# A depthwise convolution's taps on TensorE: one full product per tap, or four products of 32 channels for four taps, on shifted copies

## The chip, the core and the metric

The program runs on one core of a Trainium2 chip. The metric is the time of one execution on the device in microseconds (us), from start to end; less is better. A core has TensorE (PE in the rows; its weight loads are PEld), VectorE (DVE), ScalarE (ACT), GpSimd (POOL) and SyncE (SP), each with its own instruction stream, and DMA queues that move data between DRAM and the on-chip memories SBUF and PSUM, both of 128 partitions.

## The reference

Four layers (A, B, C, D) run one after the other on 336 tokens: 64 of a running stream and 272 of a new one. The change is in layer D, a Conformer convolution module of 2048 channels with 31 taps, and in the step that ends the program.

```python
def conformer_mixer(u, w_in, conv_w, conv_b, ln_g, ln_b, w_out, buf):
    a, b, g = jnp.split(u @ w_in, 3, axis=-1)
    v = a * jax.nn.sigmoid(b)
    ext = jnp.concatenate([buf.astype(v.dtype), v], axis=1)
    new_buf = ext[:, -(D_CONV - 1):]
    c = causal_dwconv(ext, conv_w, conv_b)      # 31 taps, each channel by itself
    c = jax.nn.silu(layernorm(c, ln_g, ln_b))
    y = (c * jax.nn.silu(g)) @ w_out
    return y, new_buf
# trunk: x = x + rmsnorm(y, norm_post)
```

## The kernel before

All activations are held with channels on partitions and tokens along the free dimension. A projection tile (`in_tile`) makes 128 output channels for all 336 tokens: 8 blocks of the contraction, three products each (high and low parts of weights and activations), 24 products of 128x128 by 336 columns. Each of these weight groups of 128x1024 is loaded by SP's queue into `wraw` (three buffers), rounded into `whi` by ScalarE, and its remainder `wlo` is taken by VectorE, or by GpSimd for the groups that the table `PRM["lo"]` names; `whi` and `wlo` have five buffers. A call of `tick` in the program prepares the weight group that lies some three tiles ahead.

Layer D has 16 channel tiles j of 128 channels. Iteration j of its loop makes tile `db` (ScalarE takes a tanh of it into `sig`) and tile `da`; VectorE multiplies them into `ext[j % 7]` (`dext` in the rows), which holds both streams with 30 earlier columns each, so that a convolution output has T = 366 columns. Then the loop puts TensorE's part of the convolution of tile j-2 (`conv_pe`), and as many gate tiles `dg` as `PRM["g"][j]` says. The 31 taps of a tile are split over three engines:

- TensorE takes the first `npe(j)` taps. For each, ScalarE writes a diagonal matrix (`diag`, identity times the tap), and TensorE multiplies it with a shifted window of `ext` into a PSUM tile `cv`. The operands are f32, and the rows show two passes (a weight load and a product record) for each such product.
- GpSimd takes the next `ngt(j)` taps: ScalarE scales a window (`gp` for the first, `gq` for the others), GpSimd adds them up in `gp` (`conv_pool`).
- VectorE takes the rest, in place on `cv` (`conv_dve`, a pair of tiles interleaved), then adds `gp`.

`finish` adds the bias (ScalarE, `call`) and squares (`sq`), and GpSimd sums both over the tiles into `s1`, `s2`, which two pairs of products with `onesE` turn into the layernorm's mean and square mean. After the 16 iterations stand the convolutions of tiles 14 and 15 and the remaining gate tiles; of these, 13 is made before the layernorm sums and 14 and 15 after them. What VectorE and ScalarE's taps advance at each place is set by the tables `PRM["pump"]`, `PRM["act"]` and `PRM["t"]`, so each engine's order is fixed in the program; engines wait for one another by semaphores.

The program ends in `outproj`, branch `last`: the sum of squares of the projected output gives `rstd` (ScalarE, a logarithm and an exponential), and VectorE and GpSimd compute `yg * rstd` and `x + yg` for 8 blocks, each of which SP then stores.

Layer A holds a place that will be needed: five products in a row of 128x32 matrices, which go to PSUM partitions r to r+32 in w columns, the last with 16 columns:

```python
for e, (r, c, w) in enumerate(((0, 32, 32), (0, 128, 32), (64, 192, 32), (0, 256, 32), (64, 320, 16))):
    self.mm(a[r:r + 32, c:c + w], k3[:, t, e], q3[:, t, e, :w])
```

Of the kernel before, what the change touches and what calls it, by code (L numbers as in the profile page):

```python
# [10 lines left out]
F32 = mybir.dt.float32  # L11
# [33 lines left out]
    "npe": [5, 5, 6, 6, 4, 4, 6, 3, 7, 5, 2, 6, 9, 4, 14, 5],  # L45
    "ngt": [3, 4, 6, 9, 6, 11, 6, 9, 7, 9, 8, 13, 8, 12, 4, 10],
    "act": [1, 16, 4, 77, 3],
    "pump": [[5, 10, 6, 3, 4], [6, 5, 6, 2, 7]],
# [158 lines left out]
def constants():  # L207
# [11 lines left out]
    for h in range(2):  # L219
# [6 lines left out]
        "k_tri": chunk_mask(),  # L226
    }


def pack(w, layers):  # L230
# [16 lines left out]
    a["dh"] = w["state_conformer_conv"][0, 0].T.reshape(16, 128, 30).transpose(1, 0, 2)  # L247
    lat = w["cache_mla_latent"][0, 0]
# [100 lines left out]
class Trunk:  # L349
# [161 lines left out]
    def outproj(self, i, layer, ready, close):  # L511
# [22 lines left out]
        with ExitStack() as st:  # L534
# [56 lines left out]
            if last:  # L591
                r = self.rstd(S["s"], D)
# [29 lines left out]
            if last:  # L622
                def scale(k, e):
                    e.tensor_tensor(yg[:, k], yg[:, k], r, op=OP.mult)
# [5 lines left out]
                for k in (6, 7):  # L630
                    scale(k, G)
                scale(0, V)
                scale(5, V)
                for k in range(5):
                    if k < 4:
                        scale(k + 1, V)
                    new_x(k, V)
                    if k in (1, 2, 3):
                        new_x((6, 7, 5)[k - 1], G)
                return  # L640
# [797 lines left out]
    def layer_d(self, i):  # L1438
        nc, tc, V, A, G = self.nc, self.tc, self.V, self.A, self.G
        T = 366  # L1440
        with ExitStack() as st:
# [15 lines left out]
            NPT = 8  # L1457
# [3 lines left out]
            NX = 7  # L1461
            npe = lambda j: PRM["npe"][j]
# [6 lines left out]
            V.tensor_scalar(dw, self.col("dcw", 0, DTAP * 16), 0.5, None, op0=OP.mult)  # L1469
            onesE = cp.tile([128, 128], F32, name="onesE")  # L1470
# [10 lines left out]
            def diags(j, n0):  # L1481
                d = wk.tile([128, NPT, 128], F32, name="diag")
                for n in range(n0, min(n0 + NPT, npe(j))):
                    A.activation(d[:, n - n0], self.ident, AF.Copy, scale=tap(n, j))  # L1484
                    yield
                cv[j, "dg", n0] = d
# [7 lines left out]
            def conv_pe(j):  # L1494
                c = cv[j] = pp["c"].tile([128, 512], F32, name="cv")
                for n0 in range(0, npe(j), NPT):
                    while (j, "dg", n0) not in cv:
                        pump_act(1)
                    d = cv.pop((j, "dg", n0))
                    for n in range(n0, min(n0 + NPT, npe(j))):  # L1500
                        self.mm(c[:, :T], d[:, n - n0], ext[j % NX][:, n:n + T], n == 0, n == npe(j) - 1)

# [199 lines left out]
```

## Time and profile before

| | |
|---|---|
| time before, median of 3 runs | 1330.7 us (1330.37 to 1334.92) |
| profiled execution, its own time | 1332.71 us |
| its span, first to last instruction | 1330.9 us |
| PE, DVE, ACT, POOL busy, share of the span | 95%, 70%, 62%, 26% |
| mean granted TensorE clock | 0.987 |

The profile is one execution; what its rows add up to is set against its span. Busy shares are means over all four layers; layer D's convolution takes only the stretch from 1016 to 1243 us, and its shares are read there.

### The profile page before, as it was taken

Reading aid. Unit: us, or ns where it says so; the run is one execution under the profiler, and the core shown is the slowest. Engines: PE = TensorE matmul, PEld = TensorE weight load, DVE = VectorE, ACT = ScalarE, POOL = GpSimd, SP = SyncE. Lnnn points to the kernel's source line nnn. Section 1 sums busy time; section 2 is a strip of 40 time slices with the busy share of each in tenths; the row PEclk is TensorE's granted clock in tenths of the full one; section 3 lists DMA queues with packets and bytes.
Section 4 is the critical chain, followed back from the end, with each engine's and each line's share of the span. In section 5 each row is a group of like instructions: output and inputs, shape, how many; then the busy total and the mean of one; then the engine's idle time right before and its main releaser. Section 6 shows DMA issues by size and latency. Waiting matters only on the chain.

```text
span 1330.9 us, 21343 instructions
## 1 busy us (share of the span) xinstructions
PE 1261.2 (95%) x8100; PEld 1194.0 (90%) x8100; DVE 932.3 (70%) x1727; ACT 818.8 (62%) x1560; POOL 339.6 (26%) x376
## 2 busy tenths in 40 slices
PE   5999999999999999899979999998999999999995
PEld 4999999999999999799979898887998899887895
DVE  5676666676658999956755555555647799989683
ACT  4677666667545877764554544454544878778653
POOL 0000000000002122100040000000012899999794
PEclk9999999999999999899999999899999999999998
DMA  5433333433441444344343222221342233322341
GB/s 202 134 113 110 124 119 106 137 123 103 135 143 64 145 142 141 112 144 143 110 155 104 88 88 90 77 96 40 120 142 81 94 112 111 111 96 80 100 147 64
DMA packets 48247, 151.29 MB, mean 114 GB/s; under 512 B 6432, under 2 KB 11888, under 8 KB 48144
## 3 DMA queue, kind: packets, MB, share of 16 engines
q1 hardware_dynamic: 44880, 142.70, 32.5%
q0 software_dynamic: 1504, 5.04, 1.2%
q10 hardware_dynamic: 1760, 2.19, 0.5%
q8 instruction: 63, 1.03, 0.3%
q14 instruction: 40, 0.33, 0.1%
HBM read 145.45 MB, written 4.46 MB: 113 GB/s over the span
## 4 chain that ended last, share of the span: by engine, by line
PE 60%; DVE 11%; ACT 9%; POOL 9%; issue 5%; DMA 2%; POOLq 0%; DVEq 0%; ACTq 0%
PE acc L389 33%; PE bacc L389 10%; POOL gp L1511 5%; PE o L389 3%; PE hacc L389 3%; DVE wlo L330 2%; POOL wlo L330 2%; PE y L389 2%; ACT whi L318 2%; PE sp L389 2%; DMA wraw<-in_wts_dram 2%; ACT Pp L1379 2%; PE ss L389 2%; PE misc L389 1%; PE x L389 1%
## 5 line engine op out<-in xcount | busy, mean ns | idle before, releaser
L389 PE MATMUL acc<-uh,whi 128*128 128x336 f32 x1208 | 391.2, 324 | 1.1 <-ACT vv L908 1.1
L389 PE MATMUL acc<-uh,wlo 128*128 128x336 f32 x1208 | 383.1, 317 | 5.1 <-POOL wlo L330 5.1
L389 PE MATMUL acc<-ul,whi 128*128 128x336 f32 x1208 | 382.1, 316 | 0.0
L318 ACT ACTIVATE whi<-wraw 128x1024 fp32r<-128x1024 f32 (+2 forms) x267 | 273.3, 1028 | 93.2 <-DMA wraw<-in_wts_dram 59.4
L330 DVE TENSOR_TENSOR wlo<-wraw,whi 128x1024 fp32r<-128x1024 f32 (+2 forms) x229 | 288.0, 1272 | 32.9 <-ACT whi L318 28.3
L389 PEld LDWEIGHTS acc<-uh,wlo 128*128 128x128 f32 x1208 | 226.7, 188 | 5.9 <-POOL wlo L330 5.9
L389 PEld LDWEIGHTS acc<-uh,whi 128*128 128x128 f32 x1208 | 227.5, 188 | 4.2 <-ACT vv L908 1.6
L389 PEld LDWEIGHTS acc<-ul,whi 128*128 128x128 f32 x1208 | 227.7, 189 | 2.0
L1519 DVE SCALAR_TENSOR_TENSOR cv<-dext,dw,cv 128x366 f32<-128x366 f32 x280 | 146.0, 595 | 0.7
L1511 POOL TENSOR_TENSOR gp<-gp,gq 128x366 f32<-128x366 f32 x109 | 115.9, 1064 | 22.9 <-ACT gq L1510 8.9
L614 POOL TENSOR_TENSOR x<-x,sroot 128x336 f32<-128x336 f32 x6 | 5.2, 893 | 448.6 <-ACT sroot L602 393.1
L330 POOL TENSOR_TENSOR wlo<-wraw,whi 128x1024 fp32r<-128x1024 f32 (+1 forms) x38 | 88.9, 2345 | 102.9 <-DVE sump L544 83.2
L389 PE MATMUL bacc<-oh,whi 128*128 128x336 f32 x288 | 92.1, 320 | 0.0
L389 PE MATMUL bacc<-oh,wlo 128*128 128x336 f32 x288 | 91.3, 317 | 0.0
L389 PE MATMUL bacc<-ol,whi 128*128 128x336 f32 x288 | 91.1, 316 | 0.0
L1510 ACT ACTIVATE gq<-dext,dw 128x366 f32<-128x366 f32 x109 | 61.6, 595 | 25.7 <-POOL gp L1511 25.4
L389 PE MATMUL acc<-oh,whi 128*128 128x336 f32 x192 | 62.2, 324 | 2.4 <-ACT dsg L1671 1.4
L389 PE MATMUL acc<-ol,whi 128*128 128x336 f32 x192 | 62.1, 323 | 2.4 <-DVE ol L1655 1.2
L389 PE MATMUL acc<-oh,wlo 128*128 128x336 f32 x192 | 61.7, 321 | 1.9 <-DVE wlo L330 1.8
L389 PE MATMUL cv<-dext,diag 128*128 128x366 f32 x182 | 59.0, 472 | 1.0 <-ACT diag L1484 0.9
L1379 ACT ACTIVATE Pp<-sp,mx 64x80 f32<-64x80 f32 (+4 forms) x80 | 30.0, 376 | 45.9 <-DVE mx L1377 26.0
L1228 POOL DMA_DIRECT2D uv<-in_wts_dram x8 | 5.7, 718 | 199.5 <-DVE sg L1132 117.8
(421 smaller groups left out, 2653.5 us busy)
## 6 DMA issues: line engine op xcount, KB each, us to landing
wraw<-in_wts_dram SPq DMA_DIRECT2D x243, 512.0 KB, 3.4
wraw<-in_wts_dram SPq DMA_DIRECT2D x16, 384.0 KB, 3.1
out_hg_dram<-sf SPq DMA_DIRECT2D x16, 128.0 KB, 2.0
wraw<-in_wts_dram SPq DMA_DIRECT2D x8, 256.0 KB, 2.7
ukt<-in_ukt_dram POOLq DMA_DIRECT2D x8, 256.0 KB, 3.0
uv<-in_wts_dram POOLq DMA_DIRECT2D x8, 256.0 KB, 4.3
x<-in_x_dram SPq DMA_DIRECT2D x8, 168.0 KB, 5.7
out_y_dram<-x SPq DMA_DIRECT2D x8, 168.0 KB, 1.9
```

Of the source, the lines that this page charges most:

```text
L318: self.nc.scalar.activation(hi[:, :n], self.raw[i][:, :n], AF.Copy)
L330: e.tensor_tensor(lo[:, :n], self.raw.pop(i)[:, :n], hi[:, :n].bitcast(F32), op=OP.subtract)
L389: self.PE.matmul(out, l, r, start=start, stop=stop)
L614: G.tensor_tensor(self.x[:, k], self.x[:, k], sq, op=OP.mult)
L1228: nc.gpsimd.dma_start(uv, src[:, :, 256 * (p % 2):256 * (p % 2) + 256])
L1379: A.activation(P[r0:r1, c:c + n], s[r0:r1, c:c + n], AF.Exp, scale=C_SCALE, bias=mx[r0:r1, j:j + 1], accum_out=sm[r0:r1, j:j + 1])
L1510: A.activation(q, e[:, n:n + T], AF.Copy, scale=tap(n, j))
L1511: G.tensor_tensor(cv[j, "p"], cv[j, "p"], q, op=OP.add)
L1519: V.scalar_tensor_tensor(c[:, :T], ext[j % NX][:, n:n + T], tap(n, j), c[:, :T], op0=OP.mult, op1=OP.add)
```

## The change

TensorE's taps are grouped by four. For tile j, `ext` is stored to DRAM (`store`, tile `dxt`) and read back by four DMAs (`shifts`, tile `dsh`): partition block n of `dsh` (32 partitions) holds, for each of the four 32-channel groups g, those 32 channels shifted by n columns. A product then takes a 128x32 matrix (`dcw`: four 32x32 diagonals one above the other, for taps 4m to 4m+3) and `dsh[:, g, 4m:4m+366]`, and writes the 32 partitions of group g. Four products, one for each g, make a step of four taps for all 128 channels. `PRM["npm"]` gives the steps of each tile: 52 in all (208 products, the 32nd tap zero). Tile 0 keeps the diagonals, with `nd` = 11 taps. `dcw` is made by VectorE in one instruction for a tile from the identity and the taps (`tap_tiles`); the taps' tile `dtw` is loaded once by GpSimd's queue and halved by VectorE.

The tables change with it: TensorE's taps go from 91 to 219 (11 + 208), GpSimd's from 125 to 93, VectorE's from 280 to 184; gate tiles after the loop move between the convolutions of tiles 13, 14 and 15. In the last step the exponential is written twice, to PSUM for VectorE and to SBUF for GpSimd, and VectorE's intermediate product stays in PSUM.

```diff
-    "npe": [5, 5, 6, 6, 4, 4, 6, 3, 7, 5, 2, 6, 9, 4, 14, 5],
-    "ngt": [3, 4, 6, 9, 6, 11, 6, 9, 7, 9, 8, 13, 8, 12, 4, 10],
+    "npm": [0, 2, 4, 3, 3, 2, 4, 3, 4, 4, 4, 4, 4, 4, 4, 3],
+    "ngt": [5, 5, 2, 6, 4, 7, 4, 3, 7, 7, 9, 7, 3, 9, 1, 14],
...
+            def store(j):
+                z = cv[j, "dr"] = dram.tile([128, 396], F32, name="dxt")
+                nc.sync.dma_start(z, ext[j % NX][:, :396])
+
+            def shifts(j):
...
+                e = cv[j, "e"] = ec.tile([128, 4, EL], F32, name="dsh")
+                for n in range(4):
+                    nc.sync.dma_start(e[32 * n:32 * n + 32], z[:, n:n + EL].rearrange("(g c) t -> c g t", c=32))
+
+            def tap_tiles(j):
+                n = 4 * PRM["npm"][j]
+                if n == 0:
+                    d = cv[j, "w"] = ep.tile([128, PRM["nd"], 128], F32, name="diag")
+                    for n in range(PRM["nd"]):
+                        A.activation(d[:, n], self.ident, AF.Copy, scale=tap(n, j))
+                    return
+                d = cv[j, "w"] = wk.tile([128, n, 32], F32, name="dcw")
+                V.tensor_tensor(d, id32.unsqueeze(1).to_broadcast([128, n, 32]),
+                                tw[:, j, :n].unsqueeze(2).to_broadcast([128, n, 32]), op=OP.mult)
...
-                    for n in range(n0, min(n0 + NPT, npe(j))):
-                        self.mm(c[:, :T], d[:, n - n0], ext[j % NX][:, n:n + T], n == 0, n == npe(j) - 1)
+                for m in range(last + 1):
+                    for g in range(4):
+                        self.mm(c[32 * g:32 * g + 32, :T], d[:, 4 * m + g], e[:, g, 4 * m:4 * m + T], m == 0, m == last)
...
+                rp = pf.tile([128, 512], F32, name="rend", bufs=1)[:, :NT]
+                A.activation(rp, l, AF.Exp, scale=-0.5)
+                A.activation(r, l, AF.Exp, scale=-0.5)
 
                 def new_x(k, e):
-                    e.tensor_tensor(self.x[:, k], self.x[:, k], yg[:, k], op=OP.add)
+                    t = yg[:, k] if e is G else pf.tile([128, 512], F32, name="yend")[:, :NT]
+                    e.tensor_tensor(t, yg[:, k], r if e is G else rp, op=OP.mult)
+                    e.tensor_tensor(self.x[:, k], self.x[:, k], t, op=OP.add)
                     nc.sync.dma_start(self.d["y"][:, k], self.x[:, k])
...
+                for k in range(8):
+                    new_x(k, G if k in (2, 5) else V)
```

On SP's queue in layer D, before, nothing but weight loads stands until the carried state `cc` is stored:

```order
L299 DMA wraw<-in_wts_dram 128x1024 x67
L299 DMA wraw<-in_wts_dram 128x768 x3
L1614 DMA out_cc_dram<-cc 128x960
L299 DMA wraw<-in_wts_dram 128x768 x13
L299 DMA wraw<-in_wts_dram 128x1024 x4
```

In the changed kernel, the same queue around the copy of tile 3 (`dext_10612`):

```order
L303 DMA wraw<-in_wts_dram 128x1024
L1496 DMA dxt<-dext_10612 128x396
L303 DMA wraw<-in_wts_dram 128x1024
L1504 DMA dsh<-dxt 32x4x378 x4
L303 DMA wraw<-in_wts_dram 128x1024 x2
```

A store and four reads of it stand between the weight loads once for each of tiles 1 to 15; the reads wait for the store to land, and the weight loads behind them wait in the queue.

On VectorE, where iteration 4 of layer D's loop writes its `ext` tile (`dext`, from `sig` and the projection's `acc`; the brackets tell whose semaphores an instruction waits for), before:

```order
L1519 SCALAR_TENSOR_TENSOR cv<-dext_10604,dw,cv 128x366 [waits DVE_49]
L1581 SCALAR_TENSOR_TENSOR dext_10608<-sig,acc 128x272 [waits PE_49,Activation_49]
L1582 SCALAR_TENSOR_TENSOR dext_10608<-sig,acc 128x64
L1519 SCALAR_TENSOR_TENSOR cv<-dext_10605,dw,cv 128x366 [waits DVE_49]
L1519 SCALAR_TENSOR_TENSOR cv<-dext_10604,dw,cv 128x366 [waits DVE_49]
```

and in the changed kernel:

```order
L1553 SCALAR_TENSOR_TENSOR cv<-dext_10609,dw,cv 128x366 [waits DVE_49]
L1619 SCALAR_TENSOR_TENSOR dext_10613<-sig,acc 128x272 [waits PE_49,Activation_49]
L1620 SCALAR_TENSOR_TENSOR dext_10613<-sig,acc 128x64
L1515 TENSOR_TENSOR dcw<-id_10627,dtw 128x384 [waits PE_49]
L1553 SCALAR_TENSOR_TENSOR cv<-dext_10610,dw,cv 128x366 [waits DVE_49]
```

Behind `ext` VectorE now has `dcw`, which takes the buffer of `dcw` of tile j-2 (two buffers) and so waits for TensorE's convolution of tile j-2; the taps and the `wlo` of later weight groups stand behind it.

On TensorE after the loop, before, the convolutions of tiles 14 and 15 stand together, and 144 projection products (six tiles) follow:

```order
L389 MATMUL acc<-uh,wlo 128x336
L389 MATMUL cv<-dext_10604,diag 128x366 x14
L389 MATMUL cv<-dext_10605,diag 128x366 x5
L389 MATMUL acc<-uh,whi 128x336
L389 MATMUL acc<-ul,whi 128x336
```

In the changed kernel (between the pieces only projection products, 48 of them, two tiles, in the first gap and 24, one tile, in the second):

```order
L393 MATMUL acc<-uh,wlo 128x336
L393 MATMUL cv<-dsh,dcw 32x366 x16
L393 MATMUL acc<-uh,whi 128x336
...
L393 MATMUL acc<-uh,wlo 128x336
L393 MATMUL cv<-dsh,dcw 32x366 x12
L393 MATMUL acc<-uh,whi 128x336
...
L393 MATMUL acc<-uh,wlo 128x336
L393 MATMUL cv<-s_10635,onesE 128x336
L393 MATMUL cv<-s_10636,onesE 128x336
```

The convolution of tile 15 now stands one tile ahead of the layernorm sums (`cv<-s,onesE`) instead of six.

## Rows read from the trace of the kernel before

**Rows 1.** Busy time by stretch (windows): stretch, its length, each engine's busy us, clock, DMA.

```profile
1016.00:1243.00 227.00, 220.77 (x1232) 196.15 (x1230) 202.57 (x360) 173.17 (x377) 196.36 (x167) 1.00 0.30 101
```

**Rows 2.** Groups of instructions, 1010 to 1240 us: busy, mean ns | idle ahead.

```profile
L1519 DVE SCALAR_TENSOR_TENSOR cv<-dext,dw,cv 128x366 f32<-128x366 f32 x280 | 146.0, 595 | 0.7
L1511 POOL TENSOR_TENSOR gp<-gp,gq 128x366 f32<-128x366 f32 x109 | 115.9, 1064 | 22.9 <-ACT gq L1510 8.9 <-issue 7.6
L389 PE MATMUL cv<-dext,diag 128*128 128x366 f32 x182 | 59.0, 472 | 1.0 <-ACT diag L1484 0.9
L330 POOL TENSOR_TENSOR wlo<-wraw,whi 128x1024 fp32r<-128x1024 f32 x21 | 51.5, 2456 | 9.4 <-ACT whi L318 9.4
L330 DVE TENSOR_TENSOR wlo<-wraw,whi 128x1024 fp32r<-128x1024 f32 x23 | 40.2, 1746 | 10.5 <-ACT whi L318 6.3 <-POOL gp L1511 4.2
```

**Rows 3.** Waits of TensorE, 1016 to 1243 us: total, times, longest.

```profile
PE acc L389 <- POOL wlo L330: 5.1, 3, 2.0
```

**Rows 4.** Timeline of TensorE, 1049 to 1056 us: start, length, what.

```profile
1050.47 3.85 PE L389 MATMUL cv<-dext,diag 128*128 128x366 f32 x12
```

**Rows 5.** Groups of TensorE by shape in layer A, 56.849 to 56.892 us.

```profile
L389 PE MATMUL y<-q,k 128*32 128x32 f32 x2 | 0.2, 218 | 0.0
```

**Rows 6.** The same view, 56.849 to 57.022 us.

```profile
L389 PE MATMUL y<-q,k 128*32 128x32 f32 x6 | 0.3, 203 | 0.0
...
L389 PE MATMUL y<-q,k 128*32 128x16 f32 x2 | 0.2, 190 | 0.0
```

**Rows 7.** Timeline of TensorE, the same place, 56.84 to 57.56 us.

```profile
56.67 0.28 PE L389 MATMUL y<-cum,kk 128*128 128x112 f32 x1
56.88 0.74 PE L389 MATMUL y<-q,k 128*32 128x32 f32 x14
```

**Rows 8.** Timelines of POOL, DVE and PE at layer D's start.

```profile
1024.13 0.47 POOL L1466 MEMSET dext<- 128x30 f32 x7
...
1023.34 1.54 DVE L1469 TENSOR_SCALAR dw<-vec 128x496 f32<-128x496 f32 x1
...
1026.35 1.23 DVE L330 TENSOR_TENSOR wlo<-wraw,whi 128x1024 fp32r<-128x1024 f32 x1 [1.33 <-ACT whi L318]
1028.11 0.44 DVE L1581 SCALAR_TENSOR_TENSOR dext<-sig,hacc 128x272 f32<-128x272 f32 x1 [0.54 <-ACT sig L1577]
...
1029.41 0.55 PE L389 MATMUL cv<-dext,diag 128*128 128x366 f32 x1 [0.47 <-ACT diag L1484]
```

**Rows 9.** DMA issues: count, KB each, median us from issue to landing.

```profile
wraw<-in_wts_dram SPq DMA_DIRECT2D x243, 512.0 KB, 3.4
...
out_hg_dram<-sf SPq DMA_DIRECT2D x16, 128.0 KB, 2.0
...
ukt<-in_ukt_dram POOLq DMA_DIRECT2D x8, 256.0 KB, 3.0
uv<-in_wts_dram POOLq DMA_DIRECT2D x8, 256.0 KB, 4.3
```

**Rows 10.** The chain that ended last, 1215 to 1243 us.

```profile
1218.56 22.25 PE acc L389 x144
1240.81 2.41 PE cv L389 x8
```

**Rows 11.** Timelines of DVE and ACT ahead of the layernorm sums.

```profile
1235.49 0.98 DVE L1525 TENSOR_TENSOR cv<-cv,gp 128x366 f32<-128x366 f32 x2
...
1238.01 0.49 ACT L1534 ACTIVATE sq<-call 128x336 f32<-128x336 f32 x1
```

**Rows 12.** Timeline of all engines at the program's end, 1315 to 1331 us.

```profile
1318.91 2.74 DVE L624 TENSOR_TENSOR yg<-yg,rstd 128x336 f32<-128x336 f32 x3 [7.21 <-ACT rstd L422]
...
1322.79 5.53 SPq L628 DMA_DIRECT2D out_y_dram<-x  x8
...
1326.17 0.92 DVE L627 TENSOR_TENSOR x<-x,yg 128x336 f32<-128x336 f32 x2
```

**Rows 13.** Instructions of tile `cv`: form of op, ns min/median/max, starts.

```profile
L1637 DVE TENSOR_TENSOR dt<-dt,cv x16: 503/504/505, 1245.0 to 1290.9; 128x336 f32<-128x336 f32 x16
```

More of the change, by code (lines that the diff above doesn't have):

```diff
@@ L226, in constants @@
         "k_tri": chunk_mask(),
+        "k_id32": np.ascontiguousarray(np.tile(np.eye(32, dtype=f), (4, 1))),
     }
@@ L591, in outproj @@
             if last:
-                r = self.rstd(S["s"], D)
+                l, r = self.nrm.tile([128, NT], F32, name="lnss", bufs=1), self.nrm.tile([128, NT], F32, name="rstd")
+                A.activation(l, S["s"], AF.Ln, scale=1.0 / D, bias=self.eps)
             else:
@@ L622, in outproj @@
             if last:
-                def scale(k, e):
-                    e.tensor_tensor(yg[:, k], yg[:, k], r, op=OP.mult)
+                pst = ExitStack()
+                pf = self.pool(pst, "end", 2, PSUM)
+                rp = pf.tile([128, 512], F32, name="rend", bufs=1)[:, :NT]
+                A.activation(rp, l, AF.Exp, scale=-0.5)
+                A.activation(r, l, AF.Exp, scale=-0.5)
                 def new_x(k, e):
-                    e.tensor_tensor(self.x[:, k], self.x[:, k], yg[:, k], op=OP.add)
+                    t = yg[:, k] if e is G else pf.tile([128, 512], F32, name="yend")[:, :NT]
+                    e.tensor_tensor(t, yg[:, k], r if e is G else rp, op=OP.mult)
+                    e.tensor_tensor(self.x[:, k], self.x[:, k], t, op=OP.add)
                     nc.sync.dma_start(self.d["y"][:, k], self.x[:, k])
[L630 to L639, printed above, removed]
+                for k in range(8):
+                    new_x(k, G if k in (2, 5) else V)
+                pst.close()
                 return
@@ L1455, in layer_d @@
             self.psum_pools = psum_pools
-            NPT = 8
             dh = ep.tile([128, 16, 30], F32, name="dh")
@@ L1469, in layer_d @@
             V.tensor_scalar(dw, self.col("dcw", 0, DTAP * 16), 0.5, None, op0=OP.mult)
+            tw = ep.tile([128, 16, 32], F32, name="dtw")
+            id32 = ep.tile([128, 32], F32, name="id32")
+            nc.gpsimd.dma_start(tw, self.d["dtap"])
+            nc.gpsimd.dma_start(id32, self.d["k_id32"])
+            V.tensor_scalar(tw, tw, 0.5, None, op0=OP.mult)
             onesE = cp.tile([128, 128], F32, name="onesE")
@@ L1495, in conv_pe @@
                 c = cv[j] = pp["c"].tile([128, 512], F32, name="cv")
[L1496 to L1500, printed above, removed]
-                        self.mm(c[:, :T], d[:, n - n0], ext[j % NX][:, n:n + T], n == 0, n == npe(j) - 1)
+                last = PRM["npm"][j] - 1
+                d = cv.pop((j, "w"))
+                if last < 0:
+                    for n in range(PRM["nd"]):
+                        self.mm(c[:, :T], d[:, n], ext[j % NX][:, n:n + T], n == 0, n == PRM["nd"] - 1)
+                    return
+                e = cv.pop((j, "e"))
+                for m in range(last + 1):
+                    for g in range(4):
+                        self.mm(c[32 * g:32 * g + 32, :T], d[:, 4 * m + g], e[:, g, 4 * m:4 * m + T], m == 0, m == last)
             def conv_pool(j, n):
@@ L1595, in layer_d @@
                     pump(P[4])
+            store(15)
             while len(bg) > 1:
                 pump(1)
+            for n in range(PRM["tg"][0]):
+                gtile(next(ng))
+                pump(PRM["t"][1])
+            shifts(15)
             conv_pe(14)
             pump(PRM["t"][0])
-            for _ in range(PRM["tg"]):
+            for n in range(PRM["tg"][1]):
                 gtile(next(ng))
```

38 lines of the change are left out of this document (23 added, 15 removed), and 18 rows, old and new, of the table PRM.

## The prediction

> **What bounds the kernel now.** The stretch of layer D's convolution is read first, in the view by windows: from 1016 to 1243 us TensorE is busy 220.8 of 227.0 us at a granted clock of 1.00, VectorE 202.6, GpSimd 196.4, ScalarE 173.2 [rows 1]. So TensorE is the limit there, and what its own work shrinks or grows by goes into the time nearly whole, as long as VectorE, close behind, keeps up. The view of waits tells what the missing 6 us are: 5.1 us in three places where a `wlo` that GpSimd makes came late [rows 3].
>
> Then the price of the taps. The 91 taps are 182 passes [rows 2]. In a run of 12 of them the group lasts 3.85 us, the last record 0.47 us, so a pass starts every (3.85 - 0.47) / 11 = 0.307 us [rows 2, 4]. 182 x 0.307 = 55.9 us of TensorE. VectorE's 280 taps take 146.0 us, 0.521 each; GpSimd's 109 additions 1.06 each [rows 2].
>
> **TensorE's taps.** 52 steps of four products, each product with 366 columns and two passes. If the four products of a step ran one after the other, a step would cost 8 x 0.307 = 2.46 us and the four taps as much as four full products; all hangs on whether products for different groups of 32 output partitions run at once. The kernel has one place that tells: layer A's five products with 128x32 matrices, three to partitions 0 to 31 and two to partitions 64 to 95. Five products with two passes are eight passes of 32 columns and two of 16, and the two of 16 belong to the last product. Two passes have started by 56.892 us, within 15 ns of the first start at 56.88 [rows 5, 7]. By 57.022 us both 16-column passes have started but only six of eight 32-column ones [rows 6]. So the last product, for partitions 64, overtook the one before it, for partitions 0: the two groups of partitions are served side by side, and each only keeps its own order. That speaks for a step in which each of four groups has just two passes, 2 x 0.307 = 0.61 us. The trace shows two groups at once, never four. The nearest rows bound the step: 0.61 us for four at once, 0.82 for three, 1.23 for two, 2.46 for one. I take 0.61, since the two seen did not slow each other.
>
> Changing the form of the products costs too. The last 128-column-matrix pass ahead of that place starts at 56.67, has 112 columns (0.094 us at the rate above), and the first small one starts at 56.88: 0.11 us lost [rows 7]. The Trainium skill, TensorEngine Tiling (Array Packing), Key Properties, speaks against the change here: switching the tiling mode drains the engine; the row agrees, with 0.11 us. 15 tiles with two switches each: 3.3 us.
>
> After: 11 full taps, 22 x 0.307 = 6.8; 52 x 0.614 = 31.9; 3.3. Together 42.0 against 55.9: **-13.9 us**. (With 0.82 a step -3.1, with 1.23 +18.2, with 2.46 +82.)
>
> **The other engines' share.** VectorE loses 96 taps, 50.0 us. It gains 15 `dcw`, of 256 to 512 columns: between half of a 1024-column `wlo` alone (0.6 us of 1.23) and the 1.54 of the 496-column scaling [rows 8], say 12 us; four more `wlo` in this stretch at 1.75 [rows 2], 7 us. About 172 us remain. But `dcw` of tile j waits for the convolution of j-2, which TensorE runs right behind tile `da`; that is some 2.7 us from the moment `ext` can be written, less the 0.65 us of writing it: 2 us in each of 13 iterations, 26 us. 198 us of some 210: it fits on average. Iteration by iteration, the worst are those with 20 taps and no gate tile, about 13 us of VectorE against 10 of TensorE; the next one gives the 3 us back, and the `wlo` that are queued behind lie some three tiles, 11 us, ahead of use. So I charge nothing, and hold this as what goes first if I am wrong. GpSimd loses 32 taps (34 us) and five `wlo` (5 x 2.46 = 12 us), ScalarE 80 diagonals and 32 scalings; the late `wlo` of GpSimd should mostly go: **-4 us** of the 5.1 (bounds 0 and -5.1).
>
> **The start of layer D.** GpSimd issues the load of `dtw` (256 KB) only behind its seven memsets, which end at 1024.6 [rows 8]; loads of that size on its queue land 3.0 to 4.3 us after issue [rows 9], at 1027.6 to 1028.9. VectorE reaches the halving of `dtw` at 1024.9 [rows 8] and waits; queued behind are a `wlo` and `ext` of tile 0. Halving (0.8 to 1.54), memset 0.2, `wlo` 1.23, `ext` 0.65: `ext` is there at 1030.4 to 1032.5 instead of 1028.7, and TensorE's first convolution, which started at 1029.41 [rows 8], starts at 1030.5 to 1032.6. **+2.2 us**.
>
> **Ahead of the layernorm.** Before, six tiles of 3.71 us (22.25 / 6) stood behind the last convolution and covered all that VectorE, ScalarE and GpSimd still had to do: the eight passes of the sums followed without a gap [rows 10]. Now only one tile does. Count from the end of tile 14's convolution: two tiles 7.4, tile 15's three steps 2.05, one tile 3.7: TensorE is free at 13.2. VectorE takes 9 of tile 14's taps meanwhile; when tile 15's convolution ends at 9.5, 9 taps (4.7) and two additions of `gp` (0.98 [rows 11]) remain: 15.2. The last square comes 2.0 us behind these additions (1236.47 to 1238.50 [rows 11]): 17.2, and GpSimd's sums about as late. The sums then end 2 to 4 us later than TensorE alone would: **+3 us** (up to 7, if VectorE gets to tile 14 late, as its queue still holds the pair 12 and 13).
>
> **The last step.** VectorE and GpSimd worked side by side on SBUF from 1318.91 to 1327.1 [rows 12]; VectorE's first three operations took 2.74 us beside GpSimd, its last two 0.92 alone. With one operand and the intermediate in PSUM, VectorE's rows hold 503 to 505 ns while GpSimd works [rows 13]: 12 x 0.52 = 6.2 us, to 1325.1. SP issues a store each 0.69 us (5.53 / 8 [rows 12]) and keeps up. **-2 us** (0 to -3).
>
> **Sum.** -13.9 - 4 + 2.2 + 3 - 2 = -14.7 us: 1332.7 becomes 1318.0 in the profiled execution, which lay 2.0 us over the median of the runs; for the median, 1330.7 - 14.7 = 1316.0.
>
> **Rivals.** *Slower: the groups don't run four at once.* With two at a time the step is 1.23 us, the sum -14.7 + 32.1, 1348 us. The mechanism would be that products start strictly in program order: the second pass of each waits for the first in the same partitions, and the next group's product stands behind it, so that one pass starts every 0.307 us beside another's end, four times 0.307 a step. It decides from 0.90 us a step on. Against it stands the overtaking in [rows 6]. The Trainium skill, TensorE: Matmul & The Clock Gate, Part 3 (Packing small matmuls), has this very rule, strict order of the products' starts and ends; the overtaking contradicts it. The Trainium skill, same page and section, gives a measured 2.38x for three column groups; by that a step is an estimated 0.77 us and the sum -6 us, about 1324; no run here shows three.
>
> *Three at a time* (a read or issue limit that only shows beyond two): 0.82 us a step, -14.7 + 10.8, 1327 us.
>
> *Weights late.* A store of 203 KB and 774 KB of reads now stand between the weight loads of 512 KB and 3.4 us each [rows 9]. SP holds the queue while the store lands (2.0 us for 128 KB [rows 9]) and issues five more transfers at up to 0.69 us; of the lead of 11 us the load (3.4) and the remainder (1.75 to 2.46 [rows 2, 9]) leave 5 to 6 us. Burst and slack are of one size. If twelve of the fifteen bursts cost TensorE 1 us: 1328 us.
>
> **Numbers.** All four groups at once and weights in time: 0.63, 1309 to 1322, 1316 the middle. Weights or `dcw` late: 0.13, 1322 to 1336. Three at a time: 0.08, 1327. Two or one: 0.16, 1348 and more. The range from 1308 to 1336 leaves out the last case and a few hundredths below. Runs tell changes apart from 0.5% on, 6.7 us, so faster means below 1324.0: 0.63, and a fifth of the second case, 0.66. Same (to 1337.4): 0.18. Slower: 0.16.
>
> **What would show it.** Right: 416 passes `cv<-dsh,dcw` whose tile `cv` keeps TensorE busy about 42 us in all, groups of 16 products lasting some 2.5 us; nearly no wait of TensorE for `wlo`; a gap of 2 to 3 us ahead of the first convolution and of 3 to 4 us ahead of the sums; VectorE waiting for TensorE at `dcw`; the last step ending some 6.2 us behind the exponential. Wrong: groups of 16 that last 5 us; waits of `whi` for loads, or of TensorE for `wlo`, behind each burst of `dsh`; VectorE busy without a pause and TensorE waiting for it.

## The result, and the profile after

The changed kernel takes 1319.66 us (median of 5 runs, 1315.96 to 1320.86) against 1330.7 for the kernel before beside it (1327.77 to 1334.92): ratio 0.9907, 95% interval 0.9881 to 0.9932. The prediction said 1316.0. The same kernel, timed again in another series, took 1315.13 against 1330.27, ratio 0.9886 (0.9860 to 0.9913). Series differ by a few us, so small effects below are read from stretches of the profiled executions and not from medians.

The profiled execution took 1320.86 us, its span is 1319.0 (before: 1332.71 and 1330.9). The span is cut at three events on TensorE's timeline: the end of the last projection product ahead of the first convolution group, the start of the first product for the layernorm's sums, and the end of the last product of all.

| profiled execution | to layer D's first group | to the sums | to the last product | to the end | span |
|---|---|---|---|---|---|
| before | 1028.9 | 211.7 | 77.1 | 13.2 | 1330.9 |
| after | 1028.2 | 201.8 | 78.7 | 10.3 | 1319.0 |
| after, second profile (e0) | 1024.8 | 201.7 | 76.6 | 10.3 | 1313.4 |

The second column is layer D's convolution: 9.9 and 10.0 us less. The last is the last step: 2.9 less. The first column differs by 3.3 us between two executions of the very same program, and the third by 2.1. Ahead of layer D the records have TensorE at half clock (1.2 GHz) for 27.3 us in the first profile and for 20.5 in the second; over all fourteen profiles it is 10.2 to 30.7 us, and the first column, 1021.6 to 1031.3, goes with it (correlation 0.90). So what differs in that column is not the change's doing. Where the third's difference is from is told below.

What TensorE waits for from layer D on (who waited, for whom, us in total, times, longest):

```profile
PE cv L393 <- ACT diag L1512: 3.2, 1, 3.2
PE cv L393 <- POOL s L1572: 3.1, 1, 3.1
PE cv L393 <- DMA dsh<-dxt: 1.4, 2, 1.1
```

The 5.1 us for GpSimd's `wlo` [rows 3] are gone. In their place stand a wait ahead of the first group, one ahead of the sums, and two short ones for the shifted copy.

The groups of instructions from 1010 to 1230 us (busy us, mean ns | idle ahead), which answer to [rows 2]:

```profile
L1553 DVE SCALAR_TENSOR_TENSOR cv<-dext,dw,cv 128x366 f32<-128x366 f32 x184 | 97.4, 596 | 3.5 <-PE cv L393 2.7
L393 PE MATMUL cv<-dsh,dcw 128*32 128x366 f32 x416 | 35.1, 474 | 1.4 <-DMA dsh<-dxt 1.4
L1515 DVE TENSOR_TENSOR dcw<-id,dtw 128x512 f32<-128x512 f32 (+2 forms) x15 | 11.9, 793 | 11.0 <-PE cv L393 11.0
L393 PE MATMUL cv<-dext,diag 128*128 128x366 f32 x22 | 8.6, 557 | 3.2 <-ACT diag L1512 3.2
```

416 passes one after the other, one each 0.307 us as the prediction reads them before, would be 128 us; they keep TensorE busy for 35.1. What a group costs is read from its neighbours on TensorE's timeline (start, length):

```profile
1196.56 0.32 PE L393 MATMUL acc<-uh,wlo 128*128 128x336 f32 x1
1196.81 2.67 PE L393 MATMUL cv<-dsh,dcw 128*32 128x366 f32 x32
1199.40 0.42 PE L393 MATMUL acc<-uh,whi 128*128 128x336 f32 x1
1199.66 0.32 PE L393 MATMUL acc<-ul,whi 128*128 128x336 f32 x1
```

From 1196.56 to 1199.66 are 3.10 us; two projection products at their usual distance of 0.154 are 0.31, so the four steps cost 2.79. By the same reading three steps cost 2.18 and two 1.56: 0.62 a step and 0.32 for the two changes of form.

The first group and the sums (PE), and VectorE ahead of each:

```profile
1031.39 8.62 PE L393 MATMUL cv<-dext,diag 128*128 128x366 f32 x22 [3.23 <-ACT diag L1512]
...
1220.95 2.05 PE L393 MATMUL cv<-dsh,dcw 128*32 128x366 f32 x24
...
1229.99 2.61 PE L393 MATMUL cv<-s,onesE 128*128 128x336 f32 x4 [3.09 <-POOL s L1572]
```

```profile
1029.12 0.43 DVE L1479 TENSOR_SCALAR dtw<-dtw 128x512 f32<-128x512 f32 x1 [10.19 <-DMA dtw<-in_dtap_dram]
...
1029.61 1.16 DVE L334 TENSOR_TENSOR wlo<-wraw,whi 128x1024 fp32r<-128x1024 f32 x1
1030.68 0.42 DVE L1619 SCALAR_TENSOR_TENSOR dext<-sig,hacc 128x272 f32<-128x272 f32 x1
...
1223.07 4.65 DVE L1553 SCALAR_TENSOR_TENSOR cv<-dext,dw,cv 128x366 f32<-128x366 f32 x9 [2.75 <-PE cv L393]
1227.63 0.99 DVE L1559 TENSOR_TENSOR cv<-cv,gp 128x366 f32<-128x366 f32 x2
```

At the start VectorE stands for 10.19 us at the halving of `dtw`, with a `wlo` and `dext` of tile 0 queued behind; the view names the diagonal tiles for TensorE's wait, but ScalarE writes them one by one from 1028.23 on, and what came just ahead of TensorE's start is `dext` (ended 1031.25); e2 below confirms it. At the end VectorE waits for tile 15's group, then has nine taps and two additions left, the two figures that the prediction counted with.

Both gaps are followed by a lower granted clock in this execution (windows; the number ahead of the last two is the clock):

```profile
1031.00:1035.00 4.00, 3.61 (x7) 2.15 (x8) 2.28 (x6) 4.00 (x12) 2.13 (x3) 0.57 0.68 218
...
1229.00:1236.00 7.00, 6.01 (x13) 4.19 (x14) 0.92 (x2) 3.78 (x7) 3.52 (x3) 0.52 0.21 67
```

The kernel before has no second under full clock from 1016 to 1243 us [rows 1]. The end of the program, VectorE's first and last operation and SP's stores, against [rows 12]:

```profile
1309.83 0.51 DVE L636 TENSOR_TENSOR yend<-yg,rend 128x336 f32<-128x336 f32 x1 [7.07 <-ACT rend L631]
...
1315.33 0.50 DVE L637 TENSOR_TENSOR x<-x,yend 128x336 f32<-128x336 f32 x1
...
1310.91 5.28 SPq L638 DMA_DIRECT2D out_y_dram<-x  x8
```

### The profile page after: what moved, and what is told of

It is laid out like the page before. It is cut to its first block, busy times and chain, and to the rows that moved or that the text cites. A ratio compares the mean times of both kernels' runs of the same rounds, so it can differ in the third digit from the quotient of the medians.

```text
span 1319.0 us, 21739 instructions
## 1 busy us (share of the span) xinstructions
PE 1253.4 (95%) x8356; PEld 1180.5 (89%) x8356; DVE 896.0 (68%) x1656; ACT 778.9 (59%) x1449; POOL 292.7 (22%) x337
## 3 DMA queue, kind: packets, MB, share of 16 engines
q8 instruction: 66, 1.08, 0.3%
## 4 chain that ended last, share of the span: by engine, by line
PE 67%; DVE 16%; ACT 7%; issue 3%; DMA 2%; POOL 1%; SPq 0%; ACTq 0%; DVEq 0%; POOLq 0%
PE acc L393 38%; PE bacc L393 9%; DVE wlo L334 4%; PE cv L393 3%; PE o L393 3%; PE hacc L393 3%; PE y L393 2%; PE sp L393 2%; ACT Pp L1382 2%; PE ss L393 2%; ACT whi L322 2%; DVE xc L976 1%; PE misc L393 1%; DMA wraw<-in_wts_dram 1%; DVE cv L1553 1%
## 5 line engine op out<-in xcount | busy, mean ns | idle before, releaser
L334 DVE TENSOR_TENSOR wlo<-wraw,whi 128x1024 fp32r<-128x1024 f32 (+2 forms) x237 | 292.4, 1248 | 30.0 <-ACT whi L322 29.4
L393 PEld LDWEIGHTS acc<-uh,whi 128*128 128x128 f32 x1208 | 228.4, 189 | 11.2 <-issue 3.8
L1553 DVE SCALAR_TENSOR_TENSOR cv<-dext,dw,cv 128x366 f32<-128x366 f32 x184 | 97.4, 596 | 3.5 <-PE cv L393 2.7
L1545 POOL TENSOR_TENSOR gp<-gp,gq 128x366 f32<-128x366 f32 x77 | 90.4, 1175 | 34.3 <-ACT gq L1544 30.4
L334 POOL TENSOR_TENSOR wlo<-wraw,whi 128x1024 fp32r<-128x1024 f32 (+1 forms) x30 | 67.3, 2250 | 18.2 <-ACT whi L322 18.2
L393 PEld LDWEIGHTS bacc<-ol,whi 128*128 128x128 f32 x288 | 54.2, 188 | 0.4
L393 PEld LDWEIGHTS bacc<-oh,whi 128*128 128x128 f32 x288 | 54.2, 188 | 0.4
L393 PEld LDWEIGHTS bacc<-oh,wlo 128*128 128x128 f32 x288 | 54.1, 188 | 0.0
```

The costliest lines, as they stand in the source:

```text
L334: e.tensor_tensor(lo[:, :n], self.raw.pop(i)[:, :n], hi[:, :n].bitcast(F32), op=OP.subtract)
L393: self.PE.matmul(out, l, r, start=start, stop=stop)
L1545: G.tensor_tensor(cv[j, "p"], cv[j, "p"], q, op=OP.add)
L1553: V.scalar_tensor_tensor(c[:, :T], ext[j % NX][:, n:n + T], tap(n, j), c[:, :T], op0=OP.mult, op1=OP.add)
```

## The experiments

The theory: the four groups of channels run at once, the gain is TensorE's taps, the vanished waits for `wlo` and a small part from the last step, and what is lost again stands at the two gaps (T1 in the expectations). The rivals: the lighter load of VectorE and GpSimd brought the gain (T2), or the last step did. All kernels, with their stretches as above:

| kernel | us | ratio to before (95%) | to first group | to the sums | to the last product | to the end |
|---|---|---|---|---|---|---|
| e1 last step only | 1327.69 | 0.9986 (0.9969-1.0003) | 1027.2 | 211.9 | 77.1 | 10.1 |
| e2 early taps load | 1320.24 | 0.9930 (0.9907-0.9953) | 1027.8 | 204.8 | 78.7 | 10.1 |
| e3 tile 15 earlier | 1316.19 | 0.9902 (0.9875-0.9928) | 1024.4 | 201.0 | 77.9 | 10.3 |
| e4 both | 1320.78 | 0.9933 (0.9914-0.9953) | 1029.0 | 203.4 | 78.2 | 10.1 |
| e5 by group | 1359.98 | 1.0223 (1.0208-1.0239) | 1027.4 | 243.2 | 78.3 | 10.3 |
| e6 steps twice | 1350.59 | 1.0166 (1.0143-1.0189) | 1025.4 | 234.2 | 78.0 | 10.3 |
| e10 half of DVE's taps | 1317.95 | 0.9902 (0.9880-0.9924) | 1031.3 | 200.8 | 76.6 | 10.3 |
| e9 reads ahead of load | 1315.38 | 0.9891 (0.9873-0.9909) | 1025.9 | 198.3 | 77.7 | 10.1 |
| e7 gap filled | 1317.02 | 0.9900 (0.9869-0.9931) | 1023.4 | 203.6 | 76.5 | 10.3 |
| e11 stores ahead too | 1311.18 | 0.9859 (0.9832-0.9886) | 1021.6 | 199.1 | 76.7 | 10.1 |
| e12 step more in tile 15 | 1315.43 | 0.9887 (0.9859-0.9914) | 1024.8 | 200.4 | 78.2 | 10.1 |
| e0 changed kernel again | 1315.13 | 0.9886 (0.9860-0.9913) | 1024.8 | 201.7 | 76.6 | 10.3 |

**Does TensorE set the pace? (e6, e10)** Every step twice:

```diff
                 for m in range(last + 1):
-                    for g in range(4):
-                        self.mm(..., m == 0, m == last)
+                  for z in range(2):
+                    for g in range(4):
+                        self.mm(..., m + z == 0, z == 1 and m == last)
```

> The changed kernel with every step of four products made twice (the sum then counts those taps twice). T1 (TensorE sets the pace of the whole layer, a step costs 0.614 us): 52 steps more by 0.614 = +31.9 us, to about 1351.6, which minus the gap ahead of the layernorm (the last group ends later, but all else too) may be +29 to +34. T2 (VectorE's and GpSimd's taps set the pace, and the change won by their lighter load): +20 us or less, since TensorE would have room.

Measured 1350.59, 30.9 us over the changed kernel's 1319.66; layer D's stretch is 32.4 longer (234.2 against 201.8). Each added step costs its 0.62 us and the layer has no room for it: TensorE sets the pace, and the second theory falls. A tile of four steps, now eight, on the timeline:

```profile
1056.79 5.13 PE L393 MATMUL cv<-dsh,dcw 128*32 128x366 f32 x64
```

The other side, every other of VectorE's taps left out:

```diff
-            for n in range(min(npe(j) + ngt(j) for j in js), DTAP):
+            for n in range(min(npe(j) + ngt(j) for j in js), DTAP, 2):
```

> The changed kernel with every other tap of VectorE's loop left out (140 of them or so are in the trace; half are then missing from the sum). T1 (VectorE is not what the layer waits for, but for the last tile's taps): only the gap ahead of the layernorm's sums shrinks, from 3.1 us to about 1, with the half clock behind it some 2 to 4 us less: 1315.5 to 1318. T2 (the load of VectorE and GpSimd sets the pace): 8 us or more less, under 1312.

1317.95 us, 1.7 less than the first series of the changed kernel and 2.8 more than its second, so the stretches must tell. The gap ahead of the sums goes (0.31 us), and little more: layer D's stretch is 1.0 us shorter, as a wait of 2.4 us for `dsh` of tile 1 takes part of it back. VectorE's taps matter at the layer's end alone.

```profile
1053.01 1.44 PE L393 MATMUL cv<-dsh,dcw 128*32 128x366 f32 x16 [2.39 <-DMA dsh<-dxt]
...
1232.09 1.69 PE L393 MATMUL cv<-s,onesE 128*128 128x336 f32 x4 [0.31 <-POOL s L1572]
```

**How far do products overtake? (e5)** The same products in another order:

```diff
-                for m in range(last + 1):
-                    for g in range(4):
+                for g in range(4):
+                    for m in range(last + 1):
```

> The changed kernel with the products of one tile written group after group (all steps of channels 0 to 31, then of 32 to 63, ...) in place of step after step. T1 (a product of another column group may overtake, but only among the few that stand next in the queue): a group of four steps takes clearly longer than its 2.68 us, and the kernel is slower by 15 us or more. Rival a (starts strictly in the order of the program, as the Trainium skill, page TensorE: Matmul & The Clock Gate, Part 3, has it): hardly any two products of different groups run together, 8 passes by 4 groups at some 0.3 us, 8 to 9 us for a tile of four steps, +70 to +85 us in all. Rival b (the engine looks as far ahead as it needs): 2.7 us as now and no change of the time.

1359.98 us, 40.3 over the changed kernel. Tiles of two, four and three steps on the timeline, and, in the view by groups, the passes of the four-step tile that have started within 1.25 us (1057.1 to 1058.36 us):

```profile
1048.11 1.46 PE L393 MATMUL cv<-dsh,dcw 128*32 128x366 f32 x16 [0.24 <-PE acc L393]
1057.11 6.43 PE L393 MATMUL cv<-dsh,dcw 128*32 128x366 f32 x32
1074.78 3.97 PE L393 MATMUL cv<-dsh,dcw 128*32 128x366 f32 x24
```

```profile
L393 PE MATMUL cv<-dsh,dcw 128*32 128x366 f32 x4 | 1.4, 477 | 0.0
```

Two steps last hardly longer than in the kernel's own order (1.44), three 3.97 against 2.05, four 6.43 against 2.67, so both rivals are out. In the four-step tile just four passes start in the first 1.25 us, one each 0.31 us; the next two start 6 ns apart at 1.26 us. Four records of a tile last 495 ns instead of 471; in the kernel's own order they are the four that open the tile, the first of each group. Here they start at 0, 1.26, 2.52 and 3.78 us in the four-step tile, four passes apart, and at 0, 0.65, 1.29 and 1.94 in the three-step one, two apart. All of it fits one picture: the engine takes products in program order, but holds up to four passes (two of these products) for one group of columns before it stands still. With n passes a group, the last group then starts 3 (n - 4) passes late and the tile lasts (n + 3 (n - 4)) x 0.3075: 6.15 us for 8 passes and 3.69 for 6, each plus the 0.16 by which the last record is longer, 6.31 and 3.85 against 6.43 and 3.97; with 4 passes nothing is late. The picture is argued from these rows; what they show is that the order is kept within a group of columns and not between groups, and that the look-ahead ends. Strict order of all starts, which the Trainium skill states (TensorE: Matmul & The Clock Gate, Part 3, Packing small matmuls), is not what this trace shows: by it the two-step tile could not have lasted 1.46 us. The kernel's own order goes round the four groups and never meets the limit.

**The last step alone (e1)**, the kernel before with the changed kernel's branch `last`:

```diff
-                r = self.rstd(S["s"], D)
+                l, r = self.nrm.tile(...), self.nrm.tile(...)
+                A.activation(l, S["s"], AF.Ln, scale=1.0 / D, bias=self.eps)
```

(and `new_x` as in the diff above).

> The kernel before with the new last step and nothing else. T1 (TensorE's taps are the gain, the last step is a small part): the stretch behind the last sum product shrinks from 13.95 us to about 11.1, the rest of the trace stays, so about 2.9 us less than the kernel before: about 1327.8. Rival (most of the 11 us come from the last step): 1322 or less.

The last stretch goes from 13.2 to 10.1 us, layer D's stays (211.9). The median is 1.7 us under before, with an interval that includes no change: 3 us are near what runs can tell.

**The start of the layer (e2, e9, e11).** First the loads on another queue, ahead of the memsets:

```diff
             nc.scalar.dma_start(dh, self.d["dh"])
+            nc.scalar.dma_start(tw, self.d["dtap"])
+            nc.scalar.dma_start(id32, self.d["k_id32"])
...
-            nc.gpsimd.dma_start(tw, self.d["dtap"])
-            nc.gpsimd.dma_start(id32, self.d["k_id32"])
```

> The changed kernel with the two loads of the taps issued on ScalarE's queue right behind that of dh, ahead of the memsets that stood before them on GpSimd's queue. T1 (the first group is late because the loaded taps are): TensorE's gap ahead of the first group falls from 3.55 us to under 1, there is no stretch at half clock at the start of D, and the time is 3 to 4 us less than the changed kernel's 1319.7: about 1316. Rival (the first group waits for ScalarE's diagonal tiles, as the releaser named in the row says, or for GpSimd's memsets): the gap stays above 2.5 us and the time within 1 us of 1319.7.

TensorE's gap falls from 3.23 to 0.40 us, though the diagonals start as late as in the changed kernel (within 0.1 us of the last projection's end in both), so the late `dtw` was its cause, and yet the time does not fall: layer D's stretch is 3.0 us longer. PE and SP's queue:

```profile
1028.20 7.00 PE L393 MATMUL cv<-dext,diag 128*128 128x366 f32 x22 [0.40 <-ACT diag L1512]
1048.63 2.67 PE L393 MATMUL cv<-dsh,dcw 128*32 128x366 f32 x16 [6.03 <-DMA dsh<-dxt]
```

```profile
1033.28 0.33 SPq L1496 DMA_DIRECT2D dxt<-dext  x1
1040.61 0.33 SPq L303 DMA_DIRECT2D wraw<-in_wts_dram  x1
1041.15 1.76 SPq L1504 DMA_DIRECT2D dsh<-dxt  x4
```

TensorE arrives sooner at tile 1's group, and its copy does not: a wait of 6.03 us, which then runs at half clock (16 passes in 2.67 us instead of 1.44). Between the store and its reads a weights' load holds SP's queue for 7 us until a buffer is free. In e9 (with e3's edit too) the reads of tile 1 stand ahead of that load:

```diff
                 if j:
                     store(j - 1)
+                if j == 2:
+                    shifts(1)
                 a = self.in_tile("da", j)
                 pump(P[1])
-                if j:
+                if j not in (0, 2):
                     shifts(j - 1)
```

> The two earlier edits together (early load of the taps, last group two projection tiles earlier), and in addition the shifted reads of tile 1 queued on SP right behind its store, ahead of a weights' load that waits for a buffer from 1033.8 to 1041.1 us in the changed kernel. T1 (what the early load won was lost to dsh of tile 1, which stood behind that weights' load on SP's queue): its issue comes at about 1038 in place of 1041, TensorE's wait of 5.6 us for dsh falls to 2 or less without half clock, and the time is 4 to 6 us under the kernel with both edits (1320.8): 1315 to 1317, and 3 us or more under the changed kernel. Rival (the reads wait for the store's landing, or for the bytes in flight, not for their place in the queue): the wait stays at 4 us or more and the time at 1319 or more. Rival (the weights' load that is now behind the reads comes late): a wait of TensorE for whi or wlo of 2 us or more takes its place.

1315.38: 4.3 us under the changed kernel's first series and none under its second, so the stretches must tell. Layer D's is 5.1 us under that of e4, which is the same without this edit, and 3.4 to 3.5 under the changed kernel's. The reads go out 2.45 us behind the store, tile 1 waits for nothing, and 2.76 us of the wait come back at tile 2:

```profile
1031.78 0.33 SPq L1496 DMA_DIRECT2D dxt<-dext  x1
1034.23 1.76 SPq L1504 DMA_DIRECT2D dsh<-dxt  x4
```

```profile
1041.05 1.44 PE L393 MATMUL cv<-dsh,dcw 128*32 128x366 f32 x16
1052.87 2.67 PE L393 MATMUL cv<-dsh,dcw 128*32 128x366 f32 x32 [2.76 <-DMA dsh<-dxt]
```

e11 does the same for tile 2, and puts the first stores right behind `dext`:

```diff
-                if j:
+                if j > 3:
                     store(j - 1)
-                if j == 2:
-                    shifts(1)
+                if j in (2, 3):
+                    shifts(j - 1)
                 a = self.in_tile("da", j)
                 pump(P[1])
-                if j not in (0, 2):
+                if j and j not in (2, 3):
                     shifts(j - 1)
...
                 V.scalar_tensor_tensor(e[:, 30:94], ...)
+                if j < 3:
+                    store(j)
```

> The kernel with the two earlier edits and the reads of tile 1 ahead of the weights' load, and in addition the stores of tiles 0 to 2 queued right behind the operation that makes the tile, and the reads of tile 2 ahead of the weights' load as well. T1 (each early group waits for its place on SP's queue): TensorE's wait of 2.8 us for dsh of tile 2 falls under 1, 1313 to 1314 (2 us under the 1315.4 of the kernel without it). Rival (the bytes in flight set the landing, or the next tile's reads are late in turn): a wait of 2 us or more for dsh of tile 2 or 3 remains, 1315 or more.

The median, 1311.18, is the best of all, 4.0 us under the changed kernel in the same series (1315.13), with intervals that touch (ratios 0.9832 to 0.9886 and 0.9860 to 0.9913). But 3.2 us of the profile's difference lie ahead of layer D, where both programs are alike (10.2 us at half clock there against 20.5); layer D's stretch is 2.6 us under the changed kernel's, and not under that of e9 (199.1 against 198.3). Tiles 2 and 3 now wait for nothing, and tile 4 waits 2.5 us. The view names VectorE; but the tile's four reads went out at 1064.45, as soon as their store had landed (1064.40), and the last of them landed 5.4 us after its issue, at 1071.13, just ahead of the start:

```profile
1064.45 1.75 SPq L1504 DMA_DIRECT2D dsh<-dxt  x4
...
1071.48 3.13 PE L393 MATMUL cv<-dsh,dcw 128*32 128x366 f32 x24 [2.51 <-DVE cv L1553]
```

The rival held: the next tile's reads are late in turn. What TensorE gains ahead of these tiles is not its own to keep, since the store and the reads behind it take their time.

**The end of the layer (e3, e4, e12).** Tile 15's reads earlier, and its group behind that of tile 14:

```diff
             for n in range(PRM["tg"][0]):
                 gtile(next(ng))
                 pump(PRM["t"][1])
-            shifts(15)
+                if n == 0:
+                    shifts(15)
             conv_pe(14)
             pump(PRM["t"][0])
+            conv_pe(15)
+            bg.append(conv_dve((14, 15)))
             for n in range(PRM["tg"][1]):
                 gtile(next(ng))
                 pump(PRM["t"][1])
-            conv_pe(15)
-            bg.append(conv_dve((14, 15)))
```

> The changed kernel with the shifted reads of the last convolution tile issued two projection tiles earlier and its group right behind that of tile 14, so that two projection tiles more stand behind it. T1 (the layernorm's sums wait for the chain that starts at the last group): VectorE's wait of 2.75 us for that group goes, TensorE's gap ahead of the sums falls from 3.41 us to about 0.7, and if the half clock behind it comes from the gap, another 1.6 us go from the stretch behind: 1315.3 to 1317. Rival (VectorE's and GpSimd's backlog at the end sets it, not the last group): the gap stays at 3 us or more and the time at 1319 to 1320. Rival (the reads move into the way of the weights' loads or land late): a wait of TensorE for dsh or weights of 2 us or more ahead of the last groups, 1320 or more.

VectorE's wait for the last group is gone, but the gap only falls from 3.09 to 2.48 us and layer D's stretch by 0.8: this time neither size was right. VectorE works through to 1222.1 (19 taps without a pause, then the additions of `gp`), and GpSimd's sums follow. e4, this edit with e2's:

> The two edits above together on the changed kernel. T1: the two gains add, since they lie 190 us apart: 7 to 9 us less than 1319.7, about 1312, with no stretch at half clock between 1027 and 1300 us. Rival (the gain of one is given back later, since VectorE or GpSimd is what bounds the layer): less than the sum of the two single gains by 2 us or more.

1320.78: the two don't add, since e2 brings its wait (5.6 us here) along. In e12 four taps of tile 15 go from VectorE to TensorE on top of e11:

```diff
-    "npm": [0, 2, 4, 3, 3, 2, 4, 3, 4, 4, 4, 4, 4, 4, 4, 3],
+    "npm": [0, 2, 4, 3, 3, 2, 4, 3, 4, 4, 4, 4, 4, 4, 4, 4],
```

> The kernel with all these edits, and four taps of tile 15 moved from VectorE to TensorE (four steps in place of three). T1 (VectorE's 19 taps for the last two tiles set the layernorm's start): VectorE ends 4 x 0.53 = 2.1 us earlier, TensorE reaches the sums 0.6 us later, GpSimd's four sums then follow its weights' low part at about 1222.8, so the gap falls from 2.5 us to about 1: 0.8 us less in the layer, and up to 1 us more behind it if the half clock shrinks: 1312 to 1313. Rival (GpSimd's low part and sums set it, not VectorE): the gap stays at 2 us or more and the time is as without the step or 0.6 us more.

The rival: the gap stays at 2.47 us, and the median is 4.2 us over e11's; of the 5.9 us between the two profiles 3.2 lie ahead of layer D. VectorE is early now and waits for GpSimd, whose queue ahead of the sums holds two additions of `gp`, a `wlo` and then the four sums:

```profile
1218.19 2.04 POOL L1545 TENSOR_TENSOR gp<-gp,gq 128x366 f32<-128x366 f32 x2
1220.18 2.41 POOL L334 TENSOR_TENSOR wlo<-wraw,whi 128x1024 fp32r<-128x1024 f32 x1
1222.54 0.89 POOL L1572 TENSOR_TENSOR s<-s,call 128x336 f32<-128x336 f32 x1
...
1220.26 0.55 DVE L1559 TENSOR_TENSOR cv<-cv,gp 128x366 f32<-128x366 f32 x1 [1.36 <-POOL gp L1545]
```

So in the changed kernel the chain from the last group sets the gap, and 0.6 us behind that limit stands the next, GpSimd's queue; it set the gap of e3 too. A `wlo` less on GpSimd there is the next thing to try; it wasn't tried.

**The half clock (e7, e0).** Fourteen products of no use (`onesE` by `onesE`, 128 columns) in the gap ahead of the sums:

```diff
+            for n in range(14):
+                self.mm(mu[:, :128], onesE, onesE, True, True)
             self.mm(mu, onesE, s1, True, False)
```

> The changed kernel with 14 products of 128 columns (onesE by onesE, into a tile that the next product overwrites) between the last gate projection and the layernorm's sums, so that TensorE works through most of its gap of 3.1 us. T1 (the half clock from 1229.3 to 1236.1 us follows from the gap): the granted clock stays at 1.00 from there, the stretch from the first sum product to the last product falls from 78.74 us to about 77, the gap with its filling stays as long, and the time is 1.5 to 2 us less: about 1318. Rival (the half clock has another cause, such as the sums' own products): the stretch stays at 78.5 or more and the time at 1319.7.

The gap stays (the sums start 3.09 us behind the last projection) and the clock in the seven us behind it is 1.00; 76.5 us to the last product. But the half clock comes all the same, 14 us behind the start of the sums, where two waits of 0.81 and 1.08 us for ScalarE's `dsg` stand (windows):

```profile
1240.00:1242.00 2.00, 1.21 (x5) 1.21 (x6) 1.97 (x3) 1.11 (x3) 2.00 (x3) 0.74 0.64 186
1242.00:1244.00 2.00, 2.00 (x9) 2.00 (x9) 2.00 (x2) 1.78 (x3) 2.00 (x2) 0.50 0.66 206
1244.00:1246.00 2.00, 2.00 (x14) 2.00 (x13) 1.97 (x4) 0.85 (x2) 2.00 (x2) 0.91 0.51 169
```

Against the second profile of the changed kernel, which has such waits and no half clock behind them, TensorE loses 1.5 us there and makes them up before the last product. e10, with no gap ahead of its sums, has the same stretch at the same place. The theory's condition, full clock from there on, is not met. Then the changed kernel again:

> The changed kernel itself, for a comparison on the same chip with the kernels above: 1319 to 1320, with the gaps of its first profile (3.2 us ahead of the first group, 3.1 us ahead of the layernorm's sums) and both stretches at half clock again.

has the same unfilled gap of 3.09 us, and this time full clock behind it, to the last product (window of the seven us from the sums on, against 0.52 in the first profile):

```profile
1226.00:1233.00 7.00, 6.44 (x33) 5.35 (x34) 2.34 (x5) 5.75 (x11) 3.11 (x3) 1.00 0.20 59
```

Its median, 1315.13, is below e7's 1317.02 of the same series. So the filling has won nothing that these runs can show. Over all profiles: of ten with an unfilled gap of 2.5 to 3.1 us ahead of the sums, eight have half clock in the next seven us, and two, e0 and e11, have none up to the last product; of the four with no gap there or a filled one, before and e1 have none, and e7 and e10 have it 14 us later. The first group is clearer: all seven profiles with a gap of 3.2 to 3.4 us ahead of it have half clock over tile 0 (8.62 to 10.06 us for it, below e0's), and none of the seven with a gap under 0.8. A gap makes half clock likely, not certain; how long it lasts varies, and why it sometimes stays away is not shown.

```profile
1028.08 9.88 PE L393 MATMUL cv<-dext,diag 128*128 128x366 f32 x22 [3.23 <-ACT diag L1512]
```

## Why the prediction was right

Sizes in the first profile; conv groups are read between their neighbours, as above.

- *TensorE's taps, -13.9.* Right in mechanism, all four groups at once: 0.62 us a step against 0.614. A pair of changes of form costs 0.32 us instead of 0.22, so 15 tiles cost 37.0 us where 35.2 were counted. With tile 0 the convolution takes 45.8 us against 57.3 before: -11.5. Of what is missing, 1.8 us lie in these 15 tiles and 2.0 in tile 0, 1.6 of them from half clock (8.62 us in place of 7.00); that the taps before cost 1.4 more than the 55.9 counted gives part back.
- *The late `wlo`, -4.* All 5.1 us went. That GpSimd's lighter queue did it is argued from the rows, and no run changes that queue alone: its additions fall from 109 to 77, but its `wlo` from 1010 to 1240 us only from 21 to 19, where five fewer were counted.
- *The start of the layer, +2.2.* The gap went from 0.47 to 3.23 us, +2.8, from the cause named; the half clock behind it was not foreseen (9.88 us for tile 0 in the second profile).
- *The other engines' share, nothing.* Right: 15 `dcw` take 11.9 us for the 12 counted, their waits for TensorE 11.0 where 26 were allowed, and between tile 0's `dext` and the sums TensorE waits for VectorE nowhere.
- *Waits for the copy.* Charged at nothing; 1.4 us at tiles 1 and 6, and none for a copy in the second profile, where tile 0 takes longer. The rival of late weights did not come: `wraw` lands in 3.9 us where it took 3.4 [rows 9], and TensorE waits for no weights in this layer. Its mechanism, SP's queue held while a store lands, is there all the same (28.4 us in eleven waits); it hits the copies and not the weights.
- *Ahead of the layernorm, +3.* 3.1 us, and behind it 1.6 us of half clock in one execution, none in the other.
- *The last step, -2.* -2.9. VectorE's twelve operations take 6.0 us for the 6.2 counted (8.2 before); the other 0.7 lie between its last operation and the end, 3.2 us instead of 3.9, which wasn't counted.
- *The sum.* -14.7 predicted; the spans give -11.9 and -17.5 in the two profiles, the series -11.0 and -15.1. Without the first column, in which the change does nothing, the profiles give -11.2 and -13.4. That the sum comes so near is in part luck: in the first profile the taps, the copies, the half clock behind the sums and the start cost 6.0 us more than counted, and the late `wlo` and the last step give 2.0 of it back.
- *The rivals.* Two or three groups at a time are out by the 35.1 us for 416 passes (64 and 43 by their prices), and so is the estimate of 0.77 us a step. Strict order of the starts is out twice, by the kernel and by e5.

What the prediction lacked is the clock: each of the two gaps that it did foresee had a price behind it, from nothing to 3 us.

## What to carry to other kernels

A product that uses 32 of 128 columns wastes next to nothing here (0.62 us a step, where one of the four alone would take two passes of 0.307), if three others for the other columns stand directly beside it in the program, apart from 0.32 us a tile for the changes of form: order them step by step, not group by group, which cost 40 us. When a stall ahead of the bound engine is taken away, look at what that engine reaches next: a store and its reads behind a load on one queue gave the gain back tile by tile. Where a gap stays, count every queue that ends in it, GpSimd's too: taking work from the one engine named only showed the next here.

## What the runs showed of the hardware that was not expected

- Between groups of 32 output columns products overtake one another, and the look-ahead ends: e5's tiles of two, three and four steps take 1.46, 3.97 and 6.43 us. That it reaches four passes deep is the picture argued from these rows.
- Two executions of one program agree to 0.1 us over the 202 us of layer D's convolution, though not item by item (tile 0 takes 8.62 us in one and 9.88 in the other, waits for the copy 1.4 and 0). They differ by 3.3 us ahead of it, with 27.3 and 20.5 us at half clock, and by 2.1 us behind the start of the layernorm's sums, where the granted clock was 0.52 in one and 1.00 in the other for the first seven us.
- This one was expected, from [rows 13], and held: VectorE's sums and products of 336 columns with an operand in PSUM take 0.50 to 0.51 us beside a busy GpSimd; the three on SBUF took 2.74 [rows 12].
